# Seven block products in place of eight: Strassen's scheme for half of an output projection

## The chip, the cores and the metric

The kernel runs on one core of a Trainium2 chip. The metric is the time of one execution on the device in microseconds (us). A core has TensorE (PE; its weight loads are PEld), VectorE (DVE), ScalarE (ACT), GpSimd (POOL) and SyncE (SP), which here issues all transfers from and to HBM. Each engine works through its own queue in order and waits on semaphores for the others.

## The reference

Two layers of a hybrid encoder, 512 tokens (S) of width 2048 (D), all in f32. The part that matters here is the end of each layer:

```
y = concatenate([o_a, o_b], axis=-1) * silu(gate)      # o_a, o_b: (1, 512, 1024)
x = x + einsum('bse,ed->bsd', y, w_out[l])             # w_out[l]: (2048, 2048)
```

`o_a` is the output of 8 differential attention heads of width 128, `o_b` that of 8 latent attention heads of width 128 (made from low-rank q and kv latents). All attention is causal by chunks of 64 tokens. Ahead of the projection stand an RMSNorm of x, one combined input projection and the attentions; behind the second layer stands a last RMSNorm with the gain `final_norm_g`.

## The kernel before

**Numbers.** Every large product is done in three matmuls: both factors are split into a high part, rounded to the type fp32r, and the low rest, and high x high, low x high and high x low are summed in PSUM (`mm3`, matmuls at L249). For a weight the split is one ACT copy (`whi`, L195) and one DVE subtraction (`wlo`, L196), both of 128x1024, in `emit_split`.

**Weights.** All weights go through one ring in the order of the list `units`. A unit is at most 128x1024. `emit_dma` loads the next unit (two `raw` buffers), `emit_split` splits it (four buffers of each part, `BUFS`), `touch(u, ahead)` makes sure that unit u and some after it are split ahead of use, `finish(u)` gives its buffers back. A split frees a raw buffer, and the next load is issued right behind it.

**Order of the work.** The order on each engine is the order of the program. `group` makes the list of pieces of one product: a piece is one unit times one block, mostly 6 matmuls of 128x512. `mix(pieces, items)` writes the pieces out and sets the items of another stage, those of the attention, between them at even distances by their costs; `mix_at` sets items behind pieces by number. An attention head runs through `pipeline`: scores and softmax for one block of 128 queries (L523 to L531), its transposes (L309), the product with v (L620), and at the end of a head `d`, the product with the gate (L627).

**The stage in question.** `OD` is the half of the output projection that belongs to the differential heads, `OM` that of the latent heads; each has four blocks of 512 columns (c), four units of two 128-row blocks of the weight each, and four blocks of 128 tokens (b). While `OD` of block j is multiplied, the latent heads of j-1 run. Behind `OD` of block 3 comes `OM`: the activations of two heads are split by `split_y` (tiles `yhl`, L636, 128x1024), and `evac_om` adds each finished bank to the residual `xs` (L970), sums its squares on ACT (L424) and, in layer 0, stores it to `x1` once a block of columns is whole; in the last layer it multiplies it by the last gain (`fg`, L978). The heads of j = 3 run between the last 8 pieces of `OD` and the first 8 of `OM`. The last column block (`order`) finishes token blocks 0 and 1 before 2 and 3, so that the norm of the next layer (`norm_items`, at the pieces that `EDGE` gives) or the output can begin.

**Memory.** Sixteen slots of 8 KB per partition (`big`, tag B) hold the residual, the gate pages, the split activations and more; a slot is given back once its tile's last reader is done. PSUM has four banks for products (`pj`) and four for everything else (`at`).

Of the kernel before, what the change touches and what calls it, by code (L numbers as in the profile page):

```python
# [11 lines left out]
F32 = mybir.dt.float32  # L12
F32R = mybir.dt.float32r
AF = mybir.ActivationFunctionType
ALU = mybir.AluOpType
# [28 lines left out]
SQ_DVE = (0, 2)  # L44
EDGE = ((11, 13, 19, 21), (17, 23, 25, 28))
# [9 lines left out]
def tile_hybrid_trunk(ctx, tc, x, norm_g, w_in, diff_lambda, diff_subln_g, mla_q_norm_g,  # L55
# [94 lines left out]
    for l in range(DEPTH):  # L150
# [18 lines left out]
        for c in range(4):  # L169
            g["OM", c] = out_units(l, c, 8)  # L170
# [5 lines left out]
    def emit_dma():  # L176
        u = ring["dma"]
        srcs, nk, w = units[u]
        raw = rawp.tile([P, 1024], F32, tag="raw", name="raw")
        view = raw[:, :nk * w].rearrange("p (k w) -> p k w", w=w)  # L180
        for off, cw, src in srcs:
            sp.dma_start(out=view[:, :, off:off + cw], in_=src)
        raws[u] = raw
        ring["dma"] += 1
        for _ in range(min(2, len(aside))):
            aside.pop(0)()

    def emit_split():
        u = ring["split"]
        _, nk, w = units[u]  # L190
# [5 lines left out]
        nc.vector.tensor_tensor(lo[:, :n], raw[:, :n], hi[:, :n].bitcast(F32), op=ALU.subtract)  # L196
        splits[u] = (hi[:, :n].rearrange("p (k w) -> p k w", w=w), lo[:, :n].rearrange("p (k w) -> p k w", w=w))
# [44 lines left out]
    def mm3(dst, w, xx, stat_w, first, last):  # L242
# [5 lines left out]
        for t, (a, b) in enumerate(trio):  # L248
            nc.tensor.matmul(dst, lhsT=a, rhs=b, start=first and t == 0, stop=last and t == 2)  # L249
# [67 lines left out]
    with tc.manual_schedule():  # L317
# [323 lines left out]
        for l in range(DEPTH):  # L641
# [119 lines left out]
            yd, ym = {}, {}  # L761
# [186 lines left out]
            for j in range(1, 4):  # L948
                pieces = mla_proj(j, *qkv[j]) + out_pieces(("OD", j), yd, evac_acc(j))
                if j == 3:  # L950
                    load_xc(3)
                    mix(pieces[:16], pend, MIX_MLA[2])
                    tail = pieces[16:]
# [8 lines left out]
            ss_acc, fg = {}, {}  # L962
            if l + 1 == DEPTH:
                fg["t"] = B([P, D], F32, "fg")
                sp.dma_start(out=fg["t"], in_=final_norm_g.unsqueeze(0).to_broadcast([P, D]))

            def evac_om(c, l=l, ss_acc=ss_acc, fg=fg):
                def evac(b, bk):
                    a = xs[c][:, b, :]
                    nc.vector.tensor_tensor(a, bk, a, op=ALU.add)  # L970
                    if c == 0:
                        ss_acc[b] = keep.tile([P, 8], F32, tag="ssx", name="ssx")
                    sumsq(ss_acc[b], c, a)
                    if l + 1 < DEPTH:
                        if b == NSB - 1:
                            sp.dma_start(out=x1[:, c * 512:(c + 1) * 512].rearrange("(b p) c -> p b c", p=P), in_=xs[c])
                    else:
# [93 lines left out]
```

## Time and profile before

| | |
|---|---|
| median of 3 runs | 1767.19 us (1767.04 to 1767.62) |
| the profiled execution | 1766.37 us |
| its span, from the first to the last instruction | 1764.6 us |
| granted clock of TensorE, mean | 0.996 of full speed |
| busy: PE, DVE, ACT, POOL | 98%, 55%, 40%, 2% |

The span is what the profile shows of the execution; about 1.8 us lie around it. A busy share counts an engine's instructions, overlapped ones once, over the whole span. The granted clock is the share of its full 2.4 GHz that TensorE was given.

### The profile page before, as it was taken

The numbers are of one execution on the slowest core, as the hardware profiler recorded it, in microseconds if no ns is written. First come the engines' busy times: TensorE is split into PE (matmuls) and PEld (weight loads), VectorE is DVE, ScalarE is ACT, GpSimd is POOL, SyncE is SP. The second block draws the span as 40 slices with busy tenths as digits, with TensorE's granted clock in tenths as the row PEclk, the third lists the DMA queues.
The fourth block names the chain that finished last, engine by engine and source line by source line (L and its number), as shares of the span: only waits on it lengthen the run. The fifth ranks groups of instructions, "written<-read, shape, count | busy, mean of one in ns | idle before, by whom it ended". The sixth has DMA issues, their size and how long they took to land.

```text
span 1764.6 us, 23519 instructions
## 1 busy us (share of the span) xinstructions
PE 1735.2 (98%) x9245; PEld 1486.4 (84%) x9245; DVE 970.0 (55%) x1785; ACT 703.3 (40%) x1424; POOL 32.0 (2%) x53
## 2 busy tenths in 40 slices
PE   6999999999999999999999999999999999999997
PEld 4888889898888988888879898888988898888886
DVE  5425646463656774464362263654645676655554
ACT  5324434443443443333362244443543444433433
POOL 1000000000000000000000000000000000000000
PEclk9999999999999999999999999999999999999999
DMA  5552323232332432313333333332324225213223
GB/s 180 163 160 84 96 84 108 72 119 76 105 95 81 123 105 64 120 60 117 122 107 89 92 104 88 96 97 83 108 72 129 75 84 155 72 61 120 84 90 125
DMA packets 142330, 179.34 MB, mean 102 GB/s; under 512 B 16942, under 2 KB 94812, under 8 KB 142092
## 3 DMA queue, kind: packets, MB, share of 16 engines
q1 hardware_dynamic: 142220, 177.85, 33.0%
q8 instruction: 72, 1.18, 0.3%
q14 instruction: 38, 0.31, 0.1%
HBM read 169.39 MB, written 13.67 MB: 104 GB/s over the span
## 4 chain that ended last, share of the span: by engine, by line
PE 97%; ACT 1%; DVE 1%; DMA 1%; issue 0%; POOL 0%; SPq 0%; ACTq 0%; POOLq 0%; DVEq 0%
PE pj L249 84%; PE oT L620 2%; PE ov L573 2%; PE pT L309 2%; PE sc L523 2%; PE sc L493 2%; PE sc L492 2%; PE nT L309 1%; DMA xs<-in_x 1%; PE oT L309 0%; PE cT L309 0%; ACT xn L99 0%; DVE nt L457 0%; ACT whi L195 0%; ACT junk L424 0%
## 5 line engine op out<-in xcount | busy, mean ns | idle before, releaser
L196 DVE TENSOR_TENSOR wlo<-raw,whi 128x1024 fp32r<-128x1024 f32 (+1 forms) x272 | 327.5, 1211 | 298.1 <-ACT whi L195 291.9
L249 PE MATMUL pj<-hThi,whi 128*128 128x512 f32 x1024 | 410.0, 400 | 0.0
L249 PE MATMUL pj<-hThi,wlo 128*128 128x512 f32 x1024 | 400.3, 391 | 0.0
L249 PE MATMUL pj<-hTlo,whi 128*128 128x512 f32 x1024 | 399.3, 390 | 0.0
L195 ACT ACTIVATE whi<-raw 128x1024 fp32r<-128x1024 f32 (+1 forms) x272 | 282.7, 1047 | 182.2 <-PE pj L249 106.3
L249 PE MATMUL pj<-whi,yhl 128*128 128x512 f32 x1024 | 323.8, 397 | 0.0
L249 PE MATMUL pj<-whi,hThi 128*128 128x256 f32 (+2 forms) x768 | 241.4, 314 | 2.1 <-ACT hThi L99 2.1
L249 PE MATMUL pj<-whi,hTlo 128*128 128x256 f32 (+2 forms) x768 | 236.1, 307 | 0.0
L249 PE MATMUL pj<-wlo,hThi 128*128 128x256 f32 (+2 forms) x768 | 235.9, 307 | 0.0
L249 PEld LDWEIGHTS pj<-hThi,wlo 128*128 128x128 f32 x1024 | 192.2, 188 | 41.8
L249 PEld LDWEIGHTS pj<-hThi,whi 128*128 128x128 f32 x1024 | 192.7, 188 | 36.6
L249 PEld LDWEIGHTS pj<-hTlo,whi 128*128 128x128 f32 x1024 | 192.9, 188 | 35.6
L249 PEld LDWEIGHTS pj<-whi,yhl 128*128 128x128 f32 x1024 | 185.5, 188 | 34.0
L249 PE MATMUL pj<-wlo,yhl 128*128 128x512 f32 x512 | 200.6, 392 | 0.0
L509 ACT ACTIVATE s<-s,mx 128x128 f32<-128x128 f32 (+3 forms) x128 | 71.0, 555 | 300.5 <-DVE mx L507 300.5
L249 PEld LDWEIGHTS pj<-whi,hThi 128*128 128x128 f32 x768 | 147.4, 192 | 7.8 <-ACT hThi L99 2.5
L249 PEld LDWEIGHTS pj<-whi,hTlo 128*128 128x128 f32 x768 | 147.2, 192 | 5.7 <-DVE hTlo L462 0.7
L249 PEld LDWEIGHTS pj<-wlo,hThi 128*128 128x128 f32 x768 | 146.9, 191 | 5.4
L249 PEld LDWEIGHTS pj<-wlo,yhl 128*128 128x128 f32 x512 | 96.1, 188 | 21.3
L720 DVE RECIPROCAL ge<-ge 128x256 f32<-128x256 f32 x64 | 112.2, 1753 | 2.2
L503 DVE CUSTOM_DVE_ANT_0 s<-sc,bt 128x128 f32<-128x128 f32 (+3 forms) x128 | 57.1, 483 | 79.4 <-POOL bt L413 54.2
L529 ACT ACTIVATE s<-sc,mx 128x128 f32<-128x128 f32 (+1 forms) x64 | 33.8, 528 | 137.9 <-DVE mx L527 137.9
(153 smaller groups left out, 1870.2 us busy)
## 6 DMA issues: line engine op xcount, KB each, us to landing
raw<-in_w_in SPq DMA_DIRECT2D x112, 512.0 KB, 3.8
raw<-in_w_in SPq DMA_DIRECT2D x128, 256.0 KB, 3.0
raw<-in_w_out SPq DMA_DIRECT2D x64, 512.0 KB, 3.7
xs<-in_x SPq DMA_DIRECT2D x32, 256.0 KB, 5.4
bt<-btab SPq DMA_DIRECT2D x16, 512.0 KB, 5.2
btab<-vecd SPq DMA_DIRECT2D x16, 320.0 KB, 6.2
raw<-in_w_in SPq DMA_DIRECT2D x10, 480.0 KB, 3.7
raw<-in_mla_w_q_b SPq DMA_DIRECT2D x16, 256.0 KB, 3.4
```

The source lines that it names most:

```text
L195: nc.scalar.activation(hi[:, :n], raw[:, :n], AF.Copy)
L196: nc.vector.tensor_tensor(lo[:, :n], raw[:, :n], hi[:, :n].bitcast(F32), op=ALU.subtract)
L249: nc.tensor.matmul(dst, lhsT=a, rhs=b, start=first and t == 0, stop=last and t == 2)
L309: nc.tensor.transpose(dst, src, ident)
L492: nc.tensor.matmul(dst, lhsT=q[:, m], rhs=khi, start=first, stop=False)
L493: nc.tensor.matmul(dst, lhsT=q[:, m], rhs=klo, start=False, stop=True)
L503: nc.vector.tensor_tensor_reduce(out=sm_t[:, :w], in0=bk[:, :w], in1=bt[:, m, 512 - w:512], op0=ALU.add, op1=ALU.max, scale=1.0, scalar=LO ...
L509: nc.scalar.activation(s[m][:, :w], s[m][:, :w], AF.Exp, bias=mx[:, 2 + m:3 + m], accum_out=sm[:, m:m + 1])
L523: nc.tensor.matmul(bk[:, :w], lhsT=qk[:, par, q], rhs=qk[:, 2 + par, :w], start=True, stop=False)
L573: nc.tensor.matmul(bk[:, :P], lhsT=st_["pt"][:, kb * P:(kb + 1) * P], rhs=v["t"][:, kb, hp * P:(hp + 1) * P], start=kb == 0, stop=kb == qb)
L620: nc.tensor.matmul(o_["bk"][:, qb * P:(qb + 1) * P], lhsT=v["t"][:, kb, hp * P:(hp + 1) * P], rhs=st_["pt"][:, kb * P:(kb + 1) * P], start ...
L720: nc.vector.reciprocal(e[:, c], e[:, c])
```

## The change

The latent heads' half of the projection is a product of A (512 tokens x 1024) and B (1024 x 2048). It is now done as two products of A with 1024 columns each (`pr` 0 and 1). Each is cut into 2 x 2 blocks: A11 to A22 of 256 tokens x 512 (the index of the rows is half of the tokens, that of the columns the gate pages 2 and 3), B11 to B22 of 512 x 512, and the four blocks of the result come out of seven block products in place of eight (Winograd's form of Strassen's scheme): P1 = A11 B11, P2 = A12 B21, and P5, P6, P3, P7, P4 with sums and differences of blocks.

- The sums of activations (S1 to S4) are formed on GpSimd (`ya_sum`) and split into tiles `ya`, one for each product, by ACT and DVE (`ya_put`), 128x512 at a time.
- The weights of a block come as one load of 128 x (4 x 512) (`load_quad`, 1 MB, in slots of `big`). P1, P2 and P3 use a quarter as it is; the differences for P5, P6, P7 and P4 are formed on GpSimd in place, over a quarter that is no longer needed (`combine`). A unit is half of such a matrix, and a unit in the ring calls `combine` where it had a load.
- A unit is multiplied with two token blocks (r) of 128 in place of four. P1, P6 and P7 add up in one bank for each r (X), P5 and P3 in another (Y); P2 and P4 have banks of their own in the pool `at`. A chain is read when a product is done and goes on to add after that; each reading is an addition to (or subtraction from) `xs` on DVE: 8 for each r in place of 4.
- `whole` does for a finished block what `evac_om` did. In the last layer `fg` is loaded later, and the gain of blocks that are finished before it are put off (`late`).
- The attention of the last heads runs between the last 10 pieces of `OD` and the first 4 of P1; the preparation of the `ya` tiles runs between P1 and P6.

The core of the diff (in `emit_dma`, a unit whose source is "sum" now calls `combine`; in `emit_split`, `split_done` follows):

```diff
+PRODUCTS = ("P1", "P2", "P5", "P6", "P3", "P7", "P4")
...
-        for c in range(4):
-            g["OM", c] = out_units(l, c, 8)
+        for pr in range(2):
+            g["OP", pr] = [(add_unit(("sum", l, pr, name, hv), 2, 512), name, hv) for name in PRODUCTS for hv in range(2)]
...
+        t = quads[pr, i, j] = big.tile([P, 4, 512], F32, tag="B", name="wq")
+        r0, c0 = (8 + 4 * (i - 1)) * P, (2 * pr + j - 1) * 512
+        sp.dma_start(out=t, in_=w_out[l, r0:r0 + 4 * P, c0:c0 + 512].rearrange("(k p) c -> p k c", p=P))
...
+        def sub(out, a, b):
+            nc.gpsimd.tensor_tensor(out, a, b, op=ALU.subtract)
+            return out
...
+        if name == "P5":
+            return sub(q(1, 1), q(1, 2), q(1, 1))
+        if name == "P6":
+            return sub(q(1, 1), q(2, 2), q(1, 1))
+        if name == "P7":
+            t = sub(q(1, 2), q(2, 2), q(1, 2))
+            if hv == 1:
+                quads.pop((pr, 2, 2))
+                if pr == 0:
+                    load_quad(l, 1, 1, 1)
+            return t
+        t = sub(q(1, 1), q(1, 1), q(2, 1))
+        if hv == 1:
+            quads.pop((pr, 2, 1))
+            if pr == 0:
+                load_quad(l, 1, 2, 1)
+        return t
+
+    def split_done(l, pr, name, hv):
+        if hv == 1 and name in ("P7", "P4"):
+            j = 2 if name == "P7" else 1
+            quads.pop((pr, 1, j))
+            if pr == 0:
+                load_quad(l, 1, *((1, 2) if name == "P7" else (2, 2)))
...
-                    mix(pieces[:16], pend, MIX_MLA[2])
-                    tail = pieces[16:]
+                    mix(pieces[:14], pend, MIX_MLA[2])
+                    tail = pieces[14:]
...
+            def whole(c, b, l=l, ss_acc=ss_acc, fg=fg):
...
+                sumsq(ss_acc[b], c, a)
+                if l + 1 < DEPTH:
+                    if b == NSB - 1:
+                        sp.dma_start(out=x1[:, c * 512:(c + 1) * 512].rearrange("(b p) c -> p b c", p=P), in_=xs[c])
+                elif "t" in fg:
+                    gain(c, b)
+                else:
+                    late.append(lambda: gain(c, b))
...
+                acopy(hi, src)
+                nc.vector.tensor_tensor(lo, src, hi.bitcast(F32), op=ALU.subtract)
...
+                def s1():
+                    ya_put("P5", g, ya_sum("S1", g, yq(2, 1, g), yq(2, 2, g), ALU.add))
+
+                def s2():
+                    ya_put("P6", g, ya_sum("S2", g, sums.pop(("S1", g)), yq(1, 1, g), ALU.subtract))
+
+                def s3():
+                    ya_put("P7", g, ya_sum("S3", g, yq(1, 1, g), yq(2, 1, g), ALU.subtract))
+                    sums.pop(("S3", g))
+
+                def s4():
+                    ya_put("P3", g, ya_sum("S4", g, yq(1, 2, g), sums.pop(("S2", g)), ALU.subtract))
+                    sums.pop(("S4", g))
+
+                return [lambda: ya_put("P2", g, yq(1, 2, g)), s1, s2, s4, s3, lambda: ya_put("P4", g, yq(2, 2, g))]
...
+            terms = {
+                "P1": ("X", ((1, 1, ALU.add),)), "P2": ("Z", ((1, 1, ALU.add),)),
+                "P5": ("Y", ((2, 2, ALU.add),)), "P6": ("X", ((1, 2, ALU.add),)),
+                "P3": ("Y", ((1, 2, ALU.add),)), "P7": ("X", ((2, 1, ALU.add), (2, 2, ALU.add))),
+                "P4": ("W", ((2, 1, ALU.subtract),)),
+            }
...
+                    hi, lo = touch(u, 3)
...
+                    if hv == 1:
+                        for i, j, op in adds:
+                            cc, sb = 2 * pr + j - 1, 2 * (i - 1) + r
+                            a = xs[cc][:, sb, :]
+                            nc.vector.tensor_tensor(a, a, bk, op=op)
...
+                order = [(name, hv, r) for name in PRODUCTS for hv in range(2) for r in range(2)]
+                if by_row:
+                    order[20:] = [(name, hv, r) for r in range(2) for name in ("P7", "P4") for hv in range(2)]
+                return [(8, lambda a=a: piece(*a)) for a in order]
...
+            half_way = len(pend) * 3 // 5
+            mix(tail, [(0.5, lambda g=g: ya_put("P1", g, yq(1, 1, g))) for g in range(2)] + pend[:half_way], MIX_MLA[3])
+            yd.clear()
+            for i in (1, 2):
+                if (0, i, 2) not in quads:
+                    load_quad(l, 0, i, 2)
+            mix(first[:4], pend[half_way:] + even(ya_items(0)[:3]))
+            items = ya_items(1)
+            items = items[:3] + ya_items(0)[3:5] + items[3:5] + ya_items(0)[5:] + items[5:]
+            items.insert(7, lambda: gates.pop(2))
+            items.append(lambda: gates.pop(3))
+            items[0]()
+            mix(first[4:16], even(items[1:]), (0.0, 0.6))
...
+            mix(first[16:], even(late))
+            second = pair_pieces(1, l + 1 == DEPTH)
+            mix(second[:12], [])
...
-                pieces = group(g["OM", 3], NSB, mm_S(act_y(ym), 512), evac_om(3), order)
+                pieces = second[12:]
```

## Rows read from the trace of the kernel before

**Rows 1.** The page: busy time by engine (1), the chain by engine and line (4).
```profile
PE 1735.2 (98%) x9245; PEld 1486.4 (84%) x9245; DVE 970.0 (55%) x1785; ACT 703.3 (40%) x1424; POOL 32.0 (2%) x53
...
PE 97%; ACT 1%; DVE 1%; DMA 1%; issue 0%; POOL 0%; SPq 0%; ACTq 0%; POOLq 0%; DVEq 0%
PE pj L249 84%; PE oT L620 2%; PE ov L573 2%; PE pT L309 2%; PE sc L523 2%; PE sc L493 2%; PE sc L492 2%; PE nT L309 1%; DMA xs<-in_x 1%; PE oT L309 0%; PE cT L309 0%; ACT xn L99 0%; DVE nt L457 0%; ACT whi L195 0%; ACT junk L424 0%
```

**Rows 2.** The chain in order of time: start, length, engine, instructions.
```profile
810.19 69.19 PE pj L249 x305
...
1677.64 77.58 PE pj L249 x342
```

**Rows 3.** Windows of the stage in layer 0: busy time, granted clock, DMA.
```profile
840.00:860.00 20.00, 20.00 (x90) 16.57 (x89) 7.28 (x8) 5.97 (x11) 0.00 (x0) 1.00 0.46 152
sum 40.00, PE 40.00 PEld 33.11 DVE 14.25 ACT 13.22 POOL 0.00; mean PE 20.00 PEld 16.56 DVE 7.13 ACT 6.61 POOL 0.00
```

**Rows 4.** Groups by line and shape: busy us, mean ns of one, idle before.
```profile
L196 DVE TENSOR_TENSOR wlo<-raw,whi 128x1024 fp32r<-128x1024 f32 x260 | 315.2, 1219 | 278.6 <-ACT whi L195 272.4 <-PE pj L249 2.4 <-DMA raw<-in_mla_w_q_b 0.6
L970 DVE TENSOR_TENSOR xs<-pj,xs 128x512 f32<-128x512 f32 x32 | 22.0, 687 | 23.5 <-PE pj L249 23.5
...
L195 ACT ACTIVATE whi<-raw 128x1024 fp32r<-128x1024 f32 x260 | 271.9, 1053 | 170.2 <-PE pj L249 104.7 <-DMA raw<-in_w_in 25.2 <-DMA raw<-in_w_out 16.6
L424 ACT ACTIVATE junk<-xs 128x512 f32<-128x512 f32 x40 | 25.2, 630 | 61.3 <-DVE xs L970 57.7 <-DMA xs<-in_x 3.4
L99 ACT ACTIVATE hThi<-nt 128x512 fp32r<-128x512 f32 x32 | 20.0, 632 | 27.2 <-DVE nt L457 27.2
L99 ACT ACTIVATE pt<-pT 128x512 f32<-128x512 f32 x32 | 18.9, 592 | 38.8 <-PE pT L309 38.8
...
masks.py:199 POOL TENSOR_SCALAR_AFFINE_SELECT ident<-ident 128x128 f32<-128x128 f32 x1 | 0.3, 292 | 0.1
L321 POOL MEMSET mhalf<- 128x8 f32 x1 | 0.1, 104 | 0.0
```

**Rows 5.** Timeline of DVE in the last layer: start, length, instruction, [idle before].
```profile
1687.37 0.69 DVE L978 TENSOR_TENSOR xs<-xs,fg 128x512 f32<-128x512 f32 x1 [0.79 <-ACT junk L424]
1687.98 0.68 DVE L970 TENSOR_TENSOR xs<-pj,xs 128x512 f32<-128x512 f32 x1
...
1694.57 2.36 DVE L196 TENSOR_TENSOR wlo<-raw,whi 128x1024 fp32r<-128x1024 f32 x2 [0.26 <-ACT whi L195]
```

**Rows 6.** Timeline of GpSimd at the start of the kernel.
```profile
7.37 0.55 POOL L314 TENSOR_TENSOR rs<-tot,mhalf 128x1 f32<-128x1 f32 x1 [6.02 <-DVE gcol L363]
15.83 1.63 POOL L314 TENSOR_TENSOR rs<-tot,mhalf 128x1 f32<-128x1 f32 x1 [7.91 <-DVE tot L313]
23.45 0.93 POOL L314 TENSOR_TENSOR rs<-tot,mhalf 128x1 f32<-128x1 f32 x1 [6.00 <-DVE tot L313]
```

**Rows 7.** Timeline of DVE at the same time.
```profile
15.82 1.23 DVE L196 TENSOR_TENSOR wlo<-raw,whi 128x1024 fp32r<-128x1024 f32 x1
```

**Rows 8.** Timeline of PE, end of the last heads' attention in layer 0.
```profile
799.97 1.02 PE L523 MATMUL sc<-qkm 128*128 128x512 f32 x2
...
807.00 0.70 PE L249 MATMUL pj<-whi,yhl 128*128 128x512 f32 x2
...
809.95 0.70 PE L249 MATMUL pj<-whi,yhl 128*128 128x512 f32 x2
```

**Rows 9.** DMA issues: KB each, median us from issue to landing.
```profile
raw<-in_w_out SPq DMA_DIRECT2D x64, 512.0 KB, 3.7
...
fg<-in_final_norm_g SPq DMA_DIRECT2D x1, 1024.0 KB, 6.6
```

**Rows 10.** Timeline of PE at the boundary of the layers.
```profile
894.38 1.73 PE L309 MATMUL nT<-ident,xn 128*128 128x128 f32 x8 [2.23 <-ACT xn L99]
```

**Rows 11.** Windows of 4 us at the boundary, columns as in rows 3.
```profile
892.00:896.00 4.00, 1.77 (x10) 1.42 (x10) 2.23 (x4) 3.09 (x6) 0.62 (x2) 0.87 0.70 262
896.00:900.00 4.00, 4.00 (x15) 3.16 (x15) 3.21 (x4) 3.24 (x5) 0.00 (x0) 0.70 0.49 135
```

## What the change will do to the time, predicted before it ran

> **What bounds the kernel now.** I read the page first: TensorE (PE) is busy 98% of the span and holds 97% of the chain that ended last, 84% of it in the one matmul line of the projections [rows 1]. A busy PE is not yet PE at its rate, so I read the rate from the chain in order of time: inside the output projection 305 matmuls take 69.19 us in layer 0, and 342 take 77.58 us in layer 1, both 0.2268 us for one of 128x512 [rows 2]. (The mean that a view by groups gives counts what overlapping matmuls share twice.) The windows of that stage then show how much cover there is: in 40 us PE is busy for 40.00, VectorE (DVE) for 14.25, ScalarE (ACT) for 13.22, GpSimd (POOL) for nothing, at a granted clock of 1.00 [rows 3]. So every matmul less is time, as long as DVE, ACT and POOL, which are given more work, keep up.
>
> **What is removed.** The latent half of the projection is 4 column blocks x 8 row blocks x 4 token blocks x 3 = 384 matmuls a layer, 87.1 us at 0.2268 us. Seven products of two pairs are 2 x 7 x 2 x 2 x 2 x 3 = 336, of the same form. 96 matmuls less in both layers: **-21.8 us**. A piece stays 6 matmuls (1.36 us); a weight unit is now used by 2 pieces instead of 4, so it lasts 2.72 us instead of 5.44.
>
> **What is added, per layer.** 12 more splits: 1.05 us on ACT, 1.22 us on DVE [rows 4]. 32 additions from PSUM instead of 16, at 0.69 us. The activations' splits become 14 of 128x512 for 4 of 128x1024: ACT 0.63, DVE 0.69. GpSimd gets 16 differences of 128x1024 and 8 sums of 128x512. Back to back, DVE starts an operation 0.61 us after one of 128x512 (1687.37 to 1687.98) and ends two of 128x1024 in 2.36 us, so 1.14 us for the first [rows 5]. DVE thus has 28 x 1.14 + 32 x 0.61 + 12 x 0.61 = 58.7 us in 336 x 0.2268 = 76.2 us of matmuls, ACT 28 x 1.05 + 16 x 0.63 (sums of squares) + 14 x 0.63 = 48.3 us [rows 4]. On average both are hidden. What decides is where the work is dense.
>
> **The price of GpSimd.** No row of before shows such a subtraction. From below: it will not be faster than DVE's 1.22 and 0.69 us. Nearest from its own engine is the affine select, 128x128 in 0.29 us [rows 4]: with the 0.10 us of a tiny memset taken off as fixed, 1.5 ns an element, so 1.6 us for 1024 and 0.86 for 512; in proportion, 2.34 and 1.17 us, my upper end. The powers of the norms take 0.55 us for one element and 1.01 for four, but that is another operation. Two inputs cost more than the select's one, so I take the middle of the upper two: 2.0 and 1.0 us. By the Trainium skill, page "GPSIMD Engine Reference", section "Performance versus the Vector engine", a subtraction of 2048 elements takes 4497 ns, an estimate of 2.25 and 1.12 us here; no run yet shows it, and with it the sum below would come out 2 us later.
>
> **Does it hold up DVE?** The trace has one hint. At 15.83 us a power that elsewhere takes 0.55 us takes 1.63, and ends 0.41 us after the DVE split that began at 15.82; the one at 23.45 takes 0.93 [rows 6, 7]. So GpSimd waits while DVE reads two SBUF operands. Whether DVE waits for GpSimd isn't shown, since the powers read almost nothing. The Trainium skill, page "SBUF — State Buffer", section "SBUF: two separate sides", says that it does: the port pair is an exclusive lock for a whole instruction, against a DVE operation with two SBUF inputs. The trace agrees for the one direction; the rule for both speaks against this change, as the last rival works out from rows.
>
> **The dense places.** Number the 14 weight units of a pair u0 to u13 (P1 is u0 and u1, P2 u2 and u3, P5 u4 and u5, P6 u6 and u7).
>
> (a) The last attention is squeezed: its last two fifths now sit between four pieces, and its last two value products follow each other with no piece between the transposes and their use. In before one piece (807.00 to 808.47) covers the 0.59 us copy [rows 4, 8]. Some 0.25 us a layer: +0.5 us.
>
> (b) P2 needs the last heads. On DVE the addition of P1's last piece, queued first, waits for PE; behind it come the last gate product and the low half of P2's operand: 0.61 + 0.61 + 0.69 us after P1's last matmul, less one matmul that needs the high half alone: 1.7 to 1.8 us idle a layer, +3.6 us. In before the split of these heads had four pieces of cover.
>
> (c) P6. POOL has in its order the difference for u7 (after the split of u5, since it overwrites what that reads) and six sums. Behind each sum stands its split on ACT and DVE, and behind all these the split of u7. From the end of u5's split: 2.0 + 6 x 1.0 us on POOL, then 0.63 (ACT, last sum), 1.05 (ACT, u7), 1.22 (DVE, u7) = 10.9 us. u5's split itself ends 3 x 0.61 + 1.14 = 3.0 us after P2's start, so u7 is there at 13.9 us; PE wants it after ten pieces, 13.6 us. So 0.3 us late if the engines don't hinder each other. If they exclude each other, DVE's two-operand work of that stretch adds up to 5 x 0.61 + 1.14 = 4.2 us: 4.5 late. GpSimd's bounds make this 0 to 1.7 without exclusion (each 0.1 us on a sum counts six times) and 1.9 to 5.9 with it. One direction is shown, so I take the upper part: 4.0 us a layer, +8.0 us.
>
> (d) The last layer multiplies each finished block by the final gain: DVE waits 0.79 us for ACT's sum of squares and works 0.69 [rows 5]. From P3 to P4 of a pair DVE has 6 x 1.14 + 8 x 0.61 + 8 x 1.43 = 23.2 us (two of the eight put off from before) against 12 pieces, 16.3 us. Up to three units split ahead (8.2 us) cover it in the second pair; in the first, (c) has eaten part of that lead: +2.5 us.
>
> (e) P7 and P4, and all of the second pair in layer 0: a difference and a split are 2.0 + 1.14 = 3.1 us a unit against 2.72, so four in a row lose 1.7 us against a lead of three units. Nothing; with the lead gone, 1.7 us each time.
>
> (f) Transfers: a weight quarter is now one load of 1 MB. The nearest row, the gain's 1 MB, lands in 6.6 us, a 512 KB weight in 3.7 [rows 9]. On SP's queue each waits for its slot, in the second pair for the first pair's P7 and P4 to be read; stores of x1 and the next loads stand behind it. The quarter is split some three units (8.2 us) after it can start, so nothing; late, it would be 2 to 4 us a pair. The gain's own load now waits for a gate page; two multiplications are put off for that. Nothing, or up to 3 us. The layer boundary and the final tail keep their pieces and their order: no change.
>
> **Sum.** -21.8 + 0.5 + 3.6 + 8.0 + 2.5 = **-7.2 us**. The profiled execution took 1766.37 us for a span of 1764.6; the median of the runs is 0.8 above it. 1766.4 - 7.2 = 1759.2, **1760.0 us** on the scale of the median.
>
> **Rivals.**
> - *All hidden but (a) and (b).* GpSimd near its lower price, no exclusion. For it: DVE idle two thirds of the stage [rows 3]. Against: DVE's queue is in order, so average slack doesn't help a split behind a waiting put. -21.8 + 4.1 = -17.7: 1749.5 us.
> - *The clock goes too.* At the layer boundary PE sat idle for 2.23 us before 894.38, and the granted clock was then 0.87 and 0.70 in two windows of 4 us: (0.13 + 0.30) x 4 = 1.7 us more at full-speed value, from the 2.4 to the 1.2 GHz level [rows 10, 11]. If each idle of (b) and (c) brings that: 4 x 1.7 = 6.9 us, so -0.3: 1766.9 us, no change. Against: while PE waits for DVE a slower PE partly costs nothing.
> - *DVE and GpSimd, each waiting for the other, become the bound (slower).* First pair, two-operand work: 14 x 1.14 + 12 x 0.61 + 8 x 2.34 + 8 x 1.17 = 51.4 us, against 28 pieces (38.1 us) and the rest of the attention (9.98 us from 799.97 to 809.95 less four pieces: 4.5 us [rows 8]): 8.8 us over, in place of (c), each layer. In the last layer 8 gains a pair add 4.9 us to each pair, where the second has 16.0 + 18.7 + 4.9 = 39.6 us of 38.1. -21.8 + 4.1 + 17.6 + 4.9 + 1.5 = +6.3, and with half of the gains' waits for ACT (16 x 0.79 / 2) +12.6: 1773 to 1780 us. It decides once the stalls of a layer pass 10.9 us. For it: the wait in [rows 6]. Against: additions from PSUM (19.5 us a layer) and waits for ACT leave the port free for GpSimd.
>
> **Chances.** My forecast (1755 to 1763) 0.44; all hidden 0.12; the clock, or stalls that just cancel the gain, 0.16; slower 0.28. The measurement tells about 0.2% (3.5 us) from no change: faster 0.56, same 0.16, slower 0.28. Leaving out the outer half of the first and of the last rival, the range is 1748 to 1776.
>
> **What would show it.** The chain in order of time should have 48 matmuls less a layer in the stage, still at 0.2268 us between stalls; POOL busy some 40 us a layer more, a difference at 2.0 and a sum at 1.0 us; PE idle 1.8 us at P2's first matmul, released by DVE, and some 4 us at P6, released by a DVE split of a unit that came from GpSimd. Wrong for sure is (c) if POOL's 128x1024 takes under 1.5 or over 2.6 us, or if DVE splits that overlap it keep 1.22 us and never start late. More idle at P7 and P4, or a granted clock under 0.95 in the stage, would mean the last two rivals.

## The result, and the profile after

The change made the kernel slower: 1818.11 us, median of 5 runs (1818.00 to 1819.35), beside 1767.04 us before, also 5 runs; ratio 1.0291, 95% interval [1.0276, 1.0306]. The forecast was 1760.0 us with a range of 1748 to 1776. The profiled execution, the slowest of the five (1819.35 us), has a span of 1817.6 us, 53.0 us longer than before.

The page answers to [rows 1]: busy time by engine, then the chain by engine.

```profile
PE 1736.8 (96%) x9149; PEld 1477.8 (81%) x9149; DVE 1066.3 (59%) x1861; ACT 733.5 (40%) x1468; POOL 142.3 (8%) x101
...
PE 88%; DVE 6%; ACT 2%; issue 2%; POOL 1%; DMA 0%; ACTq 0%; SPq 0%; POOLq 0%; DVEq 0%
```

96 matmuls fewer, as intended, and the chain still shows 24 of them in 5.44 us, 0.2268 us each:

```profile
866.14 5.44 PE ow L306 x24
```

But DVE now stands in 6% of the chain. PE's share barely moved, which is why a busy share is not to be trusted here. What to read is the view of PE's waits (engine, tile and line waited for: total us, times, longest):

```profile
PE nT L366 <- ACT xn L100: 19.8, 8, 7.4
PE pj L306 <- DVE wlo L250: 15.0, 5, 5.6
PE pj L306 <- ACT whi L249: 8.9, 3, 4.2
PE gbk L419 <- DMA gsrc<-in_diff_subln_g: 6.6, 1, 6.6
PE ow L306 <- DVE ya L1050: 5.3, 2, 2.6
PE ow L306 <- ACT whi L249: 4.0, 2, 2.1
PE pT L366 <- ACT s L586: 3.1, 2, 1.5
```

All its rows add up to 68.7 us; before they were 20.0. The mean granted clock fell from 0.996 to 0.982 of 2.4 GHz: (1 - 0.982) x 1817.6 = 32.7 us lost, before 0.004 x 1764.6 = 7.1. So -21.8 (matmuls) + 48.7 (idle) + 25.6 (clock) = 52.5, nearly the 53.0 seen. The 25.6 is an upper estimate, since a low clock costs nothing while PE stands idle. A better one is PE's busy time on the page: 1736.8 us, where 1735.2 - 21.8 = 1713.4 was to be expected, so 23.4 us. With the time behind the last matmul, 2.1 us longer (11.5 for 9.4), the sum is -21.8 + 48.7 + 23.4 + 2.1 = 52.4. Where the idles lie, the timeline of PE shows (layer 0; start, length, instruction, [idle before, and what ended it]):

```profile
811.97 0.50 PE L306 MATMUL ow<-whi,ya 128*128 128x512 f32 x1 [2.63 <-DVE ya L1050]
...
825.09 0.50 PE L306 MATMUL pj<-wlo,ya 128*128 128x512 f32 x1 [1.04 <-DVE wlo L250]
...
831.87 1.22 PE L306 MATMUL pj<-whi,ya 128*128 128x512 f32 x2 [4.18 <-ACT whi L249]
838.73 0.80 PE L306 MATMUL pj<-wlo,ya 128*128 128x512 f32 x1 [5.64 <-DVE wlo L250]
...
900.39 1.97 PE L366 MATMUL nT<-ident,xn 128*128 128x128 f32 x8 [7.43 <-ACT xn L100]
909.19 1.73 PE L366 MATMUL nT<-ident,xn 128*128 128x128 f32 x8 [2.15 <-ACT xn L100]
919.27 1.62 PE L366 MATMUL nT<-ident,xn 128*128 128x128 f32 x8 [1.77 <-ACT xn L100]
```

811.97 is P2's start, the next three are P6, the last three the layer boundary, where [rows 10] had 2.23. P6 in layer 1 has 4.23 and 5.63. The windows that answer to [rows 3] and [rows 11] show what an idle brings after it (columns as there):

```profile
820.00:840.00 20.00, 9.05 (x31) 5.71 (x30) 16.96 (x12) 10.02 (x16) 14.97 (x8) 0.78 0.00 1
840.00:860.00 20.00, 20.00 (x78) 15.86 (x78) 16.50 (x19) 8.22 (x14) 3.92 (x2) 0.88 0.65 234
...
900.00:920.00 20.00, 15.70 (x57) 12.30 (x58) 10.83 (x19) 9.98 (x18) 1.10 (x2) 0.75 0.43 145
```

In the first PE works 9.05 of 20 us while DVE and GpSimd are busy most of it; in the second PE is busy throughout at a mean clock of 0.88, and does 78 matmuls where [rows 3] had 90. The third is the boundary, at a clock of 0.75. The groups (busy us, mean ns) that answer to [rows 4]:

```profile
L250 DVE TENSOR_TENSOR wlo<-raw,whi 128x1024 fp32r<-128x1024 f32 x228 | 276.4, 1219 | 234.9 <-ACT whi L249 228.2 <-PE pj L306 3.4
L250 DVE TENSOR_TENSOR wlo<-wq,whi 128x1024 fp32r<-128x1024 f32 x56 | 92.0, 1667 | 13.5 <-ACT whi L249 13.4
L208 POOL TENSOR_TENSOR wq<-wq 128x1024 f32<-128x1024 f32 x32 | 87.5, 2749 | 449.4 <-PE sc L550 348.6 <-DVE wlo L250 100.7
```

The same split of the same shape takes 1219 ns everywhere else and 1667 beside the differences; a difference takes 2749. The timelines of GpSimd and of DVE at P6 show why:

```profile
814.94 2.39 POOL L208 TENSOR_TENSOR wq<-wq 128x1024 f32<-128x1024 f32 x1 [3.57 <-DVE wlo L250]
...
826.59 1.28 POOL L1060 TENSOR_TENSOR ys<-gate,ys 128x512 f32<-128x512 f32 x1 [3.24 <-ACT junk L481]
828.50 1.27 POOL L1060 TENSOR_TENSOR ys<-gate 128x512 f32<-128x512 f32 x1 [0.63 <-DVE ya L1050]
829.73 7.87 POOL L208 TENSOR_TENSOR wq<-wq 128x1024 f32<-128x1024 f32 x3
838.76 2.75 POOL L208 TENSOR_TENSOR wq<-wq 128x1024 f32<-128x1024 f32 x1 [1.16 <-DVE wlo L250]
```

```profile
830.39 5.01 DVE L1050 TENSOR_TENSOR ya<-ys,ya 128x512 fp32r<-128x512 f32 x2 [1.37 <-ACT ya L100]
835.32 3.36 DVE L250 TENSOR_TENSOR wlo<-wq,whi 128x1024 fp32r<-128x1024 f32 x1
838.60 0.68 DVE L1050 TENSOR_TENSOR ya<-gate,ya 128x512 fp32r<-128x512 f32 x1
839.20 3.38 DVE L250 TENSOR_TENSOR wlo<-wq,whi 128x1024 fp32r<-128x1024 f32 x1
```

Two low halves that alone take 0.69 us each last 5.01 us, and the split of u7 lasts 3.36 us to 838.68, where PE's idle of 5.64 ends. The difference that u7 needs was done at 817.33. The three that DVE meets from 829.73 on are two of P7 and one of P4, products that PE comes to only after P3: the sums ahead of them in GpSimd's queue were done, so they went off at once.

The idle of 4.18 us before that has another cause. It ends with ACT's copy for u7, which stood on ACT behind the copy of the last activation sum, and GpSimd's sums were late: the last two waited 3.24 and 0.63 us for a tile. The sums take their tiles from the same four (`T`) as ACT's sums of squares, and the square that held one up waited for DVE's addition of P2 at 824.95, which stood behind the low halves on DVE. So GpSimd waited for ACT, ACT for DVE, and DVE, through ACT's copies of the sums, for GpSimd. This is read from the trace; no run with more such tiles was made.

### The profile page after: what moved, and what is told of

Its sections match the earlier page's. It is cut to its first block, busy times and chain, and to the rows that moved or that the text cites. A ratio compares the mean times of both kernels' runs of the same rounds, so it can differ in the third digit from the quotient of the medians.

```text
span 1817.6 us, 23508 instructions
## 1 busy us (share of the span) xinstructions
PE 1736.8 (96%) x9149; PEld 1477.8 (81%) x9149; DVE 1066.3 (59%) x1861; ACT 733.5 (40%) x1468; POOL 142.3 (8%) x101
## 4 chain that ended last, share of the span: by engine, by line
PE 88%; DVE 6%; ACT 2%; issue 2%; POOL 1%; DMA 0%; ACTq 0%; SPq 0%; POOLq 0%; DVEq 0%
PE pj L306 74%; DVE wlo L250 2%; PE ov L630 2%; PE pT L366 2%; PE oT L677 2%; PE sc L580 2%; PE sc L550 2%; PE sc L549 2%; DVE xs L1113 1%; PE nT L366 1%; DVE ya L1050 1%; ACT junk L481 1%; ACT whi L249 1%; PE ow L306 1%; POOL ys L1060 0%
## 5 line engine op out<-in xcount | busy, mean ns | idle before, releaser
L250 DVE TENSOR_TENSOR wlo<-raw,whi 128x1024 fp32r<-128x1024 f32 (+1 forms) x240 | 288.7, 1209 | 254.4 <-ACT whi L249 247.8
L249 ACT ACTIVATE whi<-raw 128x1024 fp32r<-128x1024 f32 (+1 forms) x240 | 249.1, 1046 | 142.9 <-PE pj L306 84.5
L306 PE MATMUL pj<-whi,yhl 128*128 128x512 f32 x512 | 164.9, 403 | 0.0
L208 POOL TENSOR_TENSOR wq<-wq 128x1024 f32<-128x1024 f32 x32 | 87.5, 2749 | 449.4 <-PE sc L550 348.6
L306 PE MATMUL pj<-whi,ya 128*128 128x512 f32 x320 | 106.4, 415 | 11.2 <-ACT whi L249 8.9
L306 PEld LDWEIGHTS pj<-whi,yhl 128*128 128x128 f32 x512 | 90.3, 189 | 14.8
L306 PE MATMUL pj<-wlo,yhl 128*128 128x512 f32 x256 | 100.6, 393 | 0.0
```

The costliest lines, as they stand in the source:

```text
L208: nc.gpsimd.tensor_tensor(out, a, b, op=ALU.subtract)
L249: nc.scalar.activation(hi[:, :n], raw[:, :n], AF.Copy)
```

## The experiments

Each was timed with runs of before on the same chip (1766.9 to 1767.3 us).

| run | median us | ratio to before, 95% |
|---|---|---|
| e1, no differences | 1780.6 | 1.0077 [1.0062, 1.0092] |
| e2, no GpSimd work | 1769.8 | 1.0021 [1.0011, 1.0030] |
| e3, differences on DVE | 1814.7 | 1.0274 [1.0257, 1.0291] |
| e4, probe in before | 1769.4 | 1.0013 [1.0003, 1.0022] |
| e5, e2 with norm earlier | 1768.9 | 1.0011 [1.0002, 1.0021] |
| e6, no P7/P4 differences | 1793.8 | 1.0156 [1.0139, 1.0173] |
| e7, no second-pair differences | 1802.6 | 1.0204 [1.0189, 1.0220] |
| e8, sums by transfers | 1841.0 | 1.0420 [1.0405, 1.0436] |
| e9, quarter differences | 1824.0 | 1.0325 [1.0309, 1.0340] |
| e10, late differences | 1823.7 | 1.0326 [1.0309, 1.0344] |
| e11, e5 with two ahead | 1769.6 | 1.0014 [1.0005, 1.0024] |
| e12, e8 with room | 1815.4 | 1.0272 [1.0255, 1.0290] |
| e13, e2 with norm later | 1770.7 | 1.0019 [1.0010, 1.0029] |
| e14, e2 with P7 second | 1767.5 | 1.0005 [0.9995, 1.0014] |
| e15, e2 with one addition | 1764.2 | 0.9987 [0.9977, 0.9996] |

**How much each part costs.** e1 leaves out the weight differences, e2 the sums of activations as well, so both multiply undifferenced operands.

```diff
 def sub(out, a, b):
-    nc.gpsimd.tensor_tensor(out, a, b, op=ALU.subtract)
     return out
...
 def ya_sum(key, g, a, b, op, sums=sums):        # e2 too
-    t = T("ys")
-    sums[key, g] = t.rearrange("p (k s) -> p k s", k=2)
-    nc.gpsimd.tensor_tensor(sums[key, g], a, b, op=op)
-    return sums[key, g]
+    sums[key, g] = a
+    return a
```

> The changed kernel, but the 32 weight differences aren't formed: P5, P6, P7 and P4 multiply the quarter as it was loaded (so the output differs). Matmuls, splits, additions, loads, the activation sums on GpSimd and every order stay. Theory (GpSimd and DVE shut each other out, and the clock falls with the stalls): the six sums in a row before P6 remain, so some 5 us of stall a layer and little loss of clock; 1758 to 1772 us. Rival 1 (the doubled rate of splits and additions on DVE and ACT is too much, GpSimd or not): it stays above 1795. Rival 2 (the order, squeezed attention and the boundary, costs most): above 1785.

> As the run without differences, and the 16 activation sums aren't formed either: each product takes the first operand of its sum (output differs). GpSimd does nothing in the stage. Theory: only what the order costs is left (1.9 us at P2's start, some 2 to 5 us at the boundary): 1750 to 1760 us, and all DVE splits at 1.22 us. Rival 1 (DVE and ACT overloaded anyway): above 1785. Rival 2 (order): 1775 to 1790.

Both came out between the two expectations. The differences are worth 1818.1 - 1780.6 = 37.5 us, the sums 10.8, and 1769.8 - (1767.0 - 21.8) = 24.6 us of the gain are lost without any arithmetic on GpSimd. That third part the theory did not have; the runs e5, e11 and e13 to e15 come back to it.

**Another engine.** e3 has the one word changed:

```diff
-    nc.gpsimd.tensor_tensor(out, a, b, op=ALU.subtract)
+    nc.vector.tensor_tensor(out, a, b, op=ALU.subtract)
```

> The changed kernel with the 32 weight differences formed by DVE in place of GpSimd, the rest the same. DVE gets 32 x 1.14 = 36.5 us more to do. Theory: a difference then takes DVE 1.14 us in place of a lock of up to 2.4 to 2.75 us, so it is faster than the changed kernel, 1770 to 1795 us. Rival 1 (DVE's load is the trouble): slower than the changed kernel, above 1825. Rival 2 (order): the same as the changed kernel within 8 us.

The time is in the range of rival 2, 3.4 us from the changed kernel, but not for that rival's reason, the order: with the same order and no differences the kernel takes 34.1 us less than this (e1). It says that the engine hardly matters. 32 differences on DVE are 39.1 us there (1222 ns each) and cost those 34.1 us: of what was put on DVE at these places, nearly every us became a us of the kernel.

**The exclusion by itself.** e4 is the kernel before with an idle GpSimd operation for 15 of the 16 weight units of the stage in each layer, of two inputs in layer 0, of one in layer 1; its result is not used.

```diff
 raw = raws.pop(u)
+if u in extra and "t" in probe:
+    if extra[u] == 0:
+        nc.gpsimd.tensor_tensor(probe["t"], raw, raw, op=ALU.subtract)
+    else:
+        nc.gpsimd.tensor_scalar(out=probe["t"], in0=raw, scalar1=1.0, scalar2=None, op0=ALU.mult)
```

> The kernel before, with one idle GpSimd operation on each raw weight of the latent half (15 a layer), written to a tile that nobody reads: in layer 0 a subtraction with two SBUF inputs, in layer 1 a multiplication by one with a single input. Theory: DVE splits that meet a GpSimd subtraction take up to 2.4 us in place of 1.22, with ends that coincide with the end of GpSimd's; less so or not at all in layer 1; the time stays within 4 us of before, since DVE is idle two thirds of the stage. Rival (the two only share bandwidth): both take longer by a constant share whenever they overlap. Rival (no contention): all splits at 1.22 us.

Timelines of the two engines, layer 0 and then layer 1:

```profile
812.24 1.90 POOL L195 TENSOR_TENSOR probe<-raw 128x1024 f32<-128x1024 f32 x1 [5.20 <-DMA raw<-in_w_out]
...
842.72 2.50 POOL L195 TENSOR_TENSOR probe<-raw 128x1024 f32<-128x1024 f32 x1 [0.89 <-DMA raw<-in_w_out]
...
1672.63 2.77 POOL L197 TENSOR_SCALAR probe<-raw 128x1024 f32<-128x1024 f32 x1 [9.50 <-DMA raw<-in_w_out]
```

```profile
813.38 1.84 DVE L201 TENSOR_TENSOR wlo<-raw,whi 128x1024 fp32r<-128x1024 f32 x1
...
842.25 1.23 DVE L201 TENSOR_TENSOR wlo<-raw,whi 128x1024 fp32r<-128x1024 f32 x1 [3.33 <-ACT whi L200]
...
1674.66 1.23 DVE L201 TENSOR_TENSOR wlo<-raw,whi 128x1024 fp32r<-128x1024 f32 x1 [0.54 <-ACT whi L200]
```

GpSimd's subtraction ends at 814.14, DVE's split at 815.22, 1.08 us after: it did its work only then. The other way, the subtraction that began at 842.72, under a split that ran to 843.48, took 2.50 us in place of 1.90 and ended 1.74 us after that split. The one-input operation runs to 1675.40, over most of a DVE split that keeps its 1.23 us. Of seven splits that met one in layer 1, five kept 1.22 to 1.23 us; the two others took 1.67 and 1.74 us, and both ended before GpSimd did. So in this kernel DVE and GpSimd excluded each other for a whole instruction when both read two SBUF operands, in both directions; and 30 operations (15 of each kind), spread over a stage that has slack, cost only 2.3 us in all.

**Which differences.** e6 leaves out those of P7 and P4, e7 those of the second pair.

```diff
-    t = sub(q(1, 2), q(2, 2), q(1, 2))      # e6, P7
+    t = q(1, 2)
...
-t = sub(q(1, 1), q(1, 1), q(2, 1))          # e6, P4
+t = q(1, 1)
...
+    if pr == 0:                             # e7, in sub
         nc.gpsimd.tensor_tensor(out, a, b, op=ALU.subtract)
```

> The changed kernel with only the differences for P5 and P6 formed; the splits of P7 and P4 read undifferenced weights of the same size. 16 of 32 differences left. Theory by stalls: the differences cost where the activations' splits are dense, at P5 and P6 of the first pair, so leaving out those of P7 and P4 gives back little: 1806 to 1814 us. Rival, each difference costs the same by shutting VectorE out: half of the 37.5 us comes back, 1799 us (1795 to 1803).

> The changed kernel with the differences of the first pair alone; the second pair's products read undifferenced weights. 16 of 32 differences left. Theory by stalls: the first pair's P5 and P6 hold most of the cost, the second pair only the longer boundary (7.43 us against 4.38 us without differences) and short waits in the last layer: 1805 to 1811 us. Rival, each difference costs the same: 1799 us (1795 to 1803).

My theory put the cost where PE stands idle. It fell: without P7's and P4's differences 24.3 us come back, more than half, and without the second pair's 15.5. The rival had each difference cost the same: e7 is in its range, e6 1.2 us below it, so P7's and P4's differences cost more than P5's and P6's. The idles at P6 are partly made by differences of later products: in e6 the idle that was 5.64 us is 0.53, with P6's own differences all there.

```profile
832.23 0.73 PE L306 MATMUL pj<-whi,ya 128*128 128x512 f32 x2 [4.22 <-ACT whi L249]
833.49 0.80 PE L306 MATMUL pj<-wlo,ya 128*128 128x512 f32 x1 [0.53 <-DVE wlo L250]
```

**Smaller or later differences.** e9 cuts each into four, e10 issues each with its split.

```diff
-    nc.gpsimd.tensor_tensor(out, a, b, op=ALU.subtract)
+    for c in range(0, 1024, 256):           # e9
+        s = slice(c, c + 256)
+        nc.gpsimd.tensor_tensor(out[:, s], a[:, s], b[:, s], op=ALU.subtract)
...
-    raws[u] = combine(*srcs[1:])            # e10, in emit_dma
+    raws[u] = combine(*srcs[1:]) if srcs[3] in ("P1", "P2", "P3") else None
...
+if raw is None:                             # e10, in emit_split
+    raw = combine(*srcs[1:])
```

> The changed kernel with each GpSimd difference of 128x1024 issued as four of 128x256; the same arithmetic, the whole result is computed. Theory A, what costs is that VectorE waits for a whole GpSimd instruction each time it meets one (two low halves in 5.01 us, a split in 3.36 us): with pieces of a quarter VectorE waits 0.6 us instead of up to 2.4 at a time and its urgent splits pass: 1790 to 1805 us. Theory B, only the total time of the exclusion counts, whatever the pieces: 1813 us or more.

> The changed kernel with each difference issued on GpSimd only when its split is issued, instead of up to the transfers' lead earlier; the whole result is computed. Theory: in the dense place at P6 three differences of later products (7.87 us back to back) no longer stand against VectorE's urgent low halves, so the idles of 4.18 and 5.64 us a layer shrink by half or more: 1800 to 1812 us. Rival: each split now waits for its own difference right ahead of it on GpSimd (2.4 us, with VectorE's exclusion more), and the lead of three units is gone: 1818 us or more.

Both are some 6 us slower than the changed kernel, as theory B and the rival had it. Groups of e9:

```profile
L210 POOL TENSOR_TENSOR wq<-wq 128x256 f32<-128x256 f32 x128 | 125.0, 1011 | 430.0 <-PE sc L552 348.6 <-DVE wlo L252 73.4 <-DMA wq<-in_w_out 8.0
L252 DVE TENSOR_TENSOR wlo<-wq,whi 128x1024 fp32r<-128x1024 f32 x56 | 76.5, 1381 | 31.2 <-ACT whi L251 31.1
```

DVE's splits are indeed quicker (1381 for 1667 ns), but a difference is now 4 x 1.01 us, so it is late itself; PE then waits 13.2 and 11.7 us for high halves (4.0 and 8.9 in the changed kernel). The waiting changed sides.

In e10 the idles at P6 are 2.97 and 4.79 us. Its edit moves a difference in the order of the program, but not in time: GpSimd's queue doesn't wait for the split beside which the difference is written. At P6 five run back to back, u7's own and behind it the four of P7 and P4:

```profile
827.43 13.98 POOL L208 TENSOR_TENSOR wq<-wq 128x1024 f32<-128x1024 f32 x5
```

Beside them u7's split on DVE still takes 3.37 us (833.03 to 836.40). So e10 added the wait of u7 for its own difference and didn't take away the others; what differences cost that are held back until they are wanted was not measured.

**Without GpSimd's arithmetic for the weights.** e8 turns the signs of one row and one column block, so that every weight combination is a pure sum, and lets transfers add the quarters up; e12 gives their descriptors 8 KB a partition for 1, paid with one of 16 large buffers. The whole result is computed.

```diff
+nc.gpsimd.dma_start(out=t[:, 2 * hv:2 * hv + 2, :], in_=w_out[l, r0:r0 + 2 * P, c0:c0 + 512].rearrange("(k p) c -> p k c", p=P), accum_op=ALU.add)
...
-PRODUCTS = ("P1", "P2", "P5", "P6", "P3", "P7", "P4")
+PRODUCTS = ("P1", "P2", "P5", "P3", "P6", "P7", "P4")
...
-big = pool("big", 16)                       # e12
+big = pool("big", 15)
```

> The changed kernel with signs of one row block and one column block turned, so that all four weight combinations are pure sums, and these sums formed by accumulating transfers on GpSimd's queue instead of by GpSimd's arithmetic; P3 stands before P6. The whole result is computed. Theory: without the arithmetic nothing shuts VectorE out, the transfers (7 instead of 4 MB a pair) come in time: as without differences, 1777 to 1785 us. Rival: the transfers land late or their issue holds up GpSimd's sums: 1795 us or more.

> The kernel with the sums formed by accumulating transfers (1841.0 us), with eight times the room for the descriptors that GpSimd writes (8 KB instead of 1 KB a partition) and 15 large buffers instead of 16, which pay for it; the whole result is computed. Theory: the transfers came 6.4 us apart because one had to end before the next could be written, and PE waited 60.5 us for the late sums; with room for several in flight they come in time and the time is that of the kernel without differences: 1777 to 1790 us. Rival: the transfers themselves take 6 us each, one after another: 1825 us or more.

e8's transfers start some 6.4 us apart (877.34, 883.89, 890.23, ...), where 8 in a pair's 38.1 us would have to come every 4.8. With room they overlap and 25.6 us come back, with one buffer fewer; that is some two fifths of e8's 60.4 us over e1. The rest stayed: 6.9 us from issue to landing (the view of DMA issues), and in e12 PE still waits 28.7 us for additions, once for 10.80:

```profile
839.31 1.19 PE L289 MATMUL pj<-whi,ya 128*128 128x512 f32 x2 [10.80 <-DVE xs L1096]
```

The wait is for an addition, in whose queue the split of a late activation sum seems to stand ahead (GpSimd waited 3.17 us to issue the transfer ahead of that sum, at 827.90); this was read, not tried. With one buffer fewer e12 is also already 4.9 us behind e8 at the last attention of layer 0 (transposes at 807.81 for 802.88). Neither theory held fully.

**The 24.6 us without GpSimd.** In e2 the timeline of PE has the attention's idle of 1.55 us, P2's of 1.75, and at the boundary

```profile
879.68 1.89 PE L365 MATMUL nT<-ident,xn 128*128 128x128 f32 x8 [4.38 <-ACT xn L100]
888.05 1.28 PE L365 MATMUL nT<-ident,xn 128*128 128x128 f32 x8 [2.91 <-ACT xn L100]
896.80 1.93 PE L365 MATMUL nT<-ident,xn 128*128 128x128 f32 x8 [2.00 <-ACT xn L100]
```

9.29 us, where before had 0.18 + 0.24 + 2.23. The five runs that go on from e2: e5 and e13 move the first two norm blocks, e11 is e5 and lets fewer splits go ahead; e14 puts P7 second in the first pair; e15 leaves out P7's second addition in the second pair of layer 0, so that the lower right blocks are finished at P5. The main lines of the edits:

```diff
-EDGE = ((11, 13, 19, 21), (17, 23, 25, 28))
+EDGE = ((9, 10, 19, 21), (17, 23, 25, 28))   # e5, e11; e13 has 13, 15
...
-hi, lo = touch(u, 3)                         # e11
+hi, lo = touch(u, 2 if l + 1 < DEPTH and pr and name in ("P7", "P4") else 3)
...
-mix(first[:4], pend[half_way:] + even(ya_items(0)[:3]))             # e14
+mix(first[:8], pend[half_way:] + even(ya_items(0)[:3]), (0.0, 0.85))
...
-for i, j, op in adds:                        # e15
+once = l + 1 < DEPTH and pr == 1
+for i, j, op in adds[:1] if once and name == "P7" else adds:
```

> The kernel without any GpSimd work (1769.8 us), with the next layer's first two norm blocks put before the products that finish two blocks each (places 9 and 10 of the last sixteen pieces instead of 11 and 13). Theory: the changed order of finished blocks is what the layer boundary pays for, since the sums of squares of P7's pieces stand on ScalarE ahead of the norm's copies. Then the idles of 4.38 and 2.91 us shrink to about 1 us together and the lowered clock behind them goes: 1760 to 1764 us. Rival: the boundary would lose the same anyway, since VectorE and ScalarE have too much to do there; the idle only moves: 1768 us or more.

> The kernel without GpSimd work and with the earlier norm blocks (1768.9 us), with splits issued two units ahead instead of three during the second pair's last two products of layer 0, so that fewer splits stand ahead of P4's additions on VectorE. Theory: the addition that came 3.7 us after its product then comes 1.2 to 2.4 us earlier and so do the norm's copies behind it: 1765.5 to 1767.5 us. Rival: nothing, since the chain from addition to square to norm is what takes the time: 1768.4 us or more.

> The kernel without GpSimd work (1769.8 us), with the next layer's first two norm blocks put after P7's last pieces (places 13 and 15 instead of 11 and 13). Theory: VectorE's and ScalarE's mutual waits at the boundary come from norm blocks standing between P7's two double additions; behind them, the additions end with their products, and the idles of 4.38, 2.91 and 2.00 us fall to 4 us or less together: 1763 to 1766 us. Rival: the boundary keeps its sum of idles, as it did with the blocks put earlier: 1768 us or more.

> The kernel without GpSimd work (1769.8 us), with P7 second in the first pair, since its activation operand needs no head of the last attention: that attention and P2's operand then have eight pieces of cover instead of four; six additions more a pair from PSUM. Theory: the idles of 1.55 us at the attention and 1.75 us at P2 go, in both layers, 6.6 us: 1762 to 1765 us. Rival: VectorE, with the added additions and the same puts, makes PE wait as much elsewhere: 1768 us or more.

> The kernel without GpSimd work (1769.8 us), with P7's second addition (into the blocks of the lower right) left out in the second pair of layer 0, so that these two blocks are finished at P5 and P7's pieces carry one addition each and no sum of squares. Theory: P7's double additions with their squares make the convoy of VectorE and ScalarE at the boundary; without them the idles of 4.38, 2.91 and 2.00 us fall to 4 us or less together and the lowered clock with them: 1761 to 1765 us. Rival: the boundary keeps its sum of idles of 8 to 9 us as in the three tries before: 1768 us or more.

Three tries (e5, e11, e13) left the boundary's idles at 9.29, 8.22 and 8.72 us, as their rivals had it: they only move. In e5 the last one alone is

```profile
895.66 1.97 PE L365 MATMUL nT<-ident,xn 128*128 128x128 f32 x8 [5.87 <-ACT xn L100]
```

and on DVE P4's first addition starts at 891.77, 4.7 us after its product's last matmul (3.7 after the start of the other block's, from which e11's expectation counts), behind two splits that waited for ScalarE, which had waited for P7's additions. e15 takes one of these away, and idles of 1.04, 2.24 and 2.01 us remain; the time falls by 5.6 us to just under before. So P7's double additions with their squares make over half of the boundary's excess; the first expectation held in the time, with 5.3 us of idle for the 4 foreseen. e14's idles at the attention and P2 fell to 0.17 and 0.69 us in layer 0, 2.4 us less, yet the time fell by only 2.3 us: 4.9 was to be expected of two layers. In layer 1 new waits for splits took back 1.2 us (3.72 for 2.54 behind P2's start); the rest is within the runs' scatter of 3 to 4 us.

## Why the prediction was wrong

1818.1 is 58.1 us above the forecast. By the traces the terms missed by: (c) 12.7 (20.7 for 8.0), (d) 7.9 (10.4 for 2.5), (a) 2.6 (3.1 for 0.5), (b) 1.7 (5.3 for 3.6); and three that the sum had at nothing: PE's longer busy time 23.4, the layer boundary 8.7, the time behind the last matmul 2.1. Together they are 59.1.

**The matmuls** (-21.8) were right: 96 fewer, at 0.2268 us between stalls.

**(a)** was 0.25 us a layer and measured 1.55. I looked at the copy behind the transposes; what is late is the softmax's result on ACT ahead of them.

**(b)** was 1.7 to 1.8 us a layer; e2 has 1.75. With GpSimd at work it is 2.63: DVE's low half of P2's operand takes 1.56 us there for 0.69.

**(c)** is the term of the sum that failed most. I priced a difference at 2.0 and a sum at 1.0 us; alone they take 2.39 (814.94 above) and 1.28, just over my upper ends, and on the mean of all 2.75. The estimate of 2.25 us by the Trainium skill, page "GPSIMD Engine Reference", section "Performance versus the Vector engine", whose figure is for an addition, was nearer to that 2.39 than my price. The exclusion in both directions was the right mechanism. But I added up DVE's work between the sums and left out what GpSimd does once the sums are done: the differences of P7 and P4 go off early, against the very low halves and the split that P6 waits for. P6 costs 1.04 + 4.18 + 5.64 = 10.9 us in layer 0 and 9.9 in layer 1, for 4.0 foreseen. e6 shows that 5.1 of it come from those later differences. The 4.18 stay in e6 (4.22): there GpSimd took 14.83 us from u7's difference to its last sum, for the 8.0 of my sum, and 3.87 of them are waits for tiles, which I had left out.

**(e)** was "nothing; with the lead gone, 1.7 us each time". P7's and P4's differences cost 24.3 us (e6), the second pair's 15.5 (e7). I had compared a unit's time with the lead of three units, and not asked whose work a waiting GpSimd instruction stands against. **(d)** was 2.5 us and is 2.5 in e2 (0.53 + 0.95 + 0.53 + 0.53, layer 1 after P6), but that is chance: I expected it between P3 and P4 of the first pair, where (c) had eaten the lead, and in e2, without (c), it lies at P1, P2 and P4 of the second pair, which I had called covered. With GpSimd the same stretch idles 10.4 us. That DVE idles two thirds of the stage [rows 3] was a bad guide: what it needs is room at the few places where it is late.

**(f)** The transfers: a quarter landed in 6.2 us (6.6 by the gain's row), and no idle names one. But "the layer boundary and the final tail: no change" was wrong. PE's boundary idles are 9.29 us without GpSimd, 11.35 with it, for 2.65; and in e2 the last matmul ends at 1755.1 us as in before, while the span ends 12.7 us later instead of 9.4. DVE's last addition starts there at 1758.44, behind P7's two (1754.92) and a gain: another 3.3 us.

**The clock** I had as a rival at 6.9 us and in the sum at nothing; it took some 23 (25.6 by the mean clock). It follows the idles: the sum of PE's waits and the clock's loss, worked out as above, are 20.0 and 7 us before, 35.2 and 9 in e2, 48.3 and 18 in e6, 58.4 and 23 in e7, 68.7 and 33 after (the clock is given to 0.001, 1.8 us).

**The rivals.** The last one, DVE and GpSimd each waiting for the other, is what happened, with stalls of 27 us in layer 0 (15.8 without the boundary's) against its deciding point of 10.9. Its 1773 to 1780 us were short, because its sum held neither the boundary nor a clock loss. Its rule, from the Trainium skill, page "SBUF — State Buffer", section "SBUF: two separate sides", says a lock for a whole instruction in both directions; e4's ends agree (1.08 us after 814.14, 1.74 us after 843.48). By that section any GpSimd operation that reads SBUF should do the same; e4's one-input operations differ from it, since five of seven splits kept their time under them, and the measurement decides. My test for (c), a difference above 2.6 us, was met.

What stays open: of e2's 24.6 us, 15.2 are idle (35.2 less 20.0: 3.1 attention, 3.5 P2, 6.6 boundary, the rest (d)), some 2 clock and 3.3 tail. PE's busy time holds most of what remains: it fell from 1735.2 to 1719.4 us, 15.8 where 96 matmuls are 21.8, so 6.0 us of longer matmuls and short gaps, of which the clock is some 2. What lengthened the rest by 4 us stays open. No version that computes the whole result came below the kernel before; e15 is 0.1% below it, with an addition left out.

## What to carry to other kernels

Before moving elementwise work to an "idle" engine, list what the engine that shares its access runs at the moment when the moved work *can* start, not when it is wanted: here early work, in order, delayed urgent work on DVE. Moving it back to DVE cost nearly the same, and cutting it finer a little more, so the question was the sum of work at the dense places, not the engine. To hold early work back, the order of the program was not enough (e10): the engine's own queue must be made to wait, and what that gives was not tried. And a trade of matmuls for vector work must pay for what those idles do to the clock, here about another half of the added idle time itself, and for evacuations that fall on the last pieces of a stage.

## What the hardware showed that I had not expected

- A one-input GpSimd operation (128x1024) took 2.78 us on the mean, longer than one with both inputs the same tile (1.99), and left five of seven DVE splits at 1.22 to 1.23 us; the two-input one made them wait for its end.
- The exclusion goes by the instruction: with quarters of 128x256 the splits took 1381 ns for 1667, while a quarter took 1011 ns on the mean, 4.0 us a difference (720 ns at the least).
- An accumulating transfer of 512 KB took GpSimd 1.2 us to issue and landed in 6.2 us (e8) to 6.9 us (e12); a plain one landed in 3.6 (e8, weights of the same matrix).
